# Bias rows formed on 128 partitions, and the indexer's narrow columns as one block, in a two-layer decoder trunk

## The chip, the cores and the metric

One Trainium2 chip, of which the program uses one core. The metric is the device time of one execution in microseconds. The time before is 1499.97 us, the median of three runs (1499.28 to 1501.76).

## The reference

Two post-norm layers on x of 256 tokens by 1024. Layer 0 mixes tokens with four heads of gated linear attention (GLA) and eight heads of sparse attention (DSA) whose keys an indexer selects, all from one input projection `w_in_ab`; a dense SwiGLU follows. Layer 1 mixes with forgetting attention and dilated attention, and ends in a top-2-of-8 expert SwiGLU. One table of relative biases (32 buckets by 8 heads) serves the DSA and the dilated heads. Cut to what the change touches:

```python
y = x @ w_in                                  # w_in_ab, 1024 x 3672
qa, ka, va, ra, ga, qb, kb, vb, qi, ki, wi = _split(y, AB_SPLITS)
g_log = jax.nn.log_sigmoid((ga @ w_gate + b_gate).astype(jnp.float32)) / GLA_GATE_TAU
...
score = jnp.einsum('bqh,bhqk->bqk', wib, jax.nn.relu(s))      # wi weighs the indexer's heads
...
bias = rel_table[_rel_bucket(tq[None, :, None] - sel)]
logits = logits + bias.transpose(0, 3, 1, 2).astype(jnp.float32)
```

Three of the parts of y are narrow: ga (16 columns, the gate's low rank), ki (64 columns, the indexer's key) and wi (8 columns, the weights of its heads). In the matrix, ki and wi stand side by side (columns 3600 to 3671); the second range that the kernel loads, columns 1512 to 1551, holds ga at its end (1536 to 1551), with 24 columns ahead of it that nobody uses.

## The kernel before

Every float32 projection is made from three matmuls (`mm3`, L188 to L190): weights and activations are each split in a high and a low half. `piece` (L151 and on) loads a block of weights into a ring of buffers named `raw` with a DMA on SP's queue, ScalarE casts it to the high half (`whi`, L160) and VectorE subtracts to get the low half (`wlo`, L162). Up to five such blocks are on their way in layer 0; a buffer comes free when the block's `wlo` is made, and the next load on SP's queue waits for that. `proj_t` makes 128 columns at a time: eight row blocks of 128, three matmuls each, so 24 matmuls of 256 columns for up to 128 weight columns.

`mixer_ab` is the first stage. In the order of its text: x is transposed, qa and ka are projected (a block of 1 MB for ka), `bias_tables` forms the bias rows, `router_weights` prepares something for the last stage, the narrow columns are projected, and then qb, qi, kb and va, interleaved with the GLA's scores, which need ga. The order in which each engine gets its instructions is made when the kernel is built, by a planner that simulates the time line; each engine then takes its instructions strictly in that order, DMA issues on its own queue among them.

`bias_tables` (L337 to L347) multiplies the table, 33 rows by 8 heads (`tb`), with a constant matrix (`oh`, 33 by 384 for each of two tables). The result has one row of 384 for each head, on 8 partitions (`row`, L346). L347 writes each row 32 times over to a buffer in DRAM (`scr_bias`), with one DMA on ScalarE's queue for each table. `bias_expand` (L356) reads it back later with four DMAs on ScalarE's queue, each row shifted by one element, into the tile `T`, which the DSA's logits add. `T` takes the place in SBUF of `oh` and `row` (tag `Tdsa`).

The narrow columns are fetched by two DMAs of L151: 72 columns (288 bytes a row) and 40 columns (160 bytes a row), for 1024 rows each, side by side in one ring buffer. `evac_small` takes ga, ki and wi out of the product.

Of the kernel before, what the change touches and what calls it, by code (L numbers as in the profile page):

```python
# [9 lines left out]
F32 = mybir.dt.float32  # L10
# [14 lines left out]
KT = 8  # L25
# [44 lines left out]

def layouts(inputs):

    cols = np.stack([inputs["ln_g"][1, 0], inputs["ln_b"][1, 0]]).reshape(2, KT, 128).transpose(2, 0, 1)
    return {"ln_cols": np.ascontiguousarray(cols)}


def drain(*gens):
    for g in gens:
        for _ in g:
            pass  # L80


def chain(*gens):
    for g in gens:
        yield from g


def interleave(main, side, n=1, m=1):

    alive = [True, True]  # L90
    while any(alive):
        for i, g, k in ((0, main, n), (1, side, m)):
            for _ in range(k):
                if alive[i] and next(g, g) is g:
                    alive[i] = False


def weave(pattern, **gens):

    for c in pattern:  # L100
        next(gens[c], None)


def lead(n, k):

    return [(t, i) for i in range(n - k) for t in range(NT)] + [(t, i) for t in range(NT) for i in range(n - k, n)]


class Trunk:
# [222 lines left out]

    def bias_tables(self, m):

        nc = self.nc
        tb = self.wk.tile([33, 8], F32, name="tb")
        nc.vector.memset(tb[32:33, :], 1.0)  # L337
        nc.gpsimd.dma_start(tb[0:32, :], self.io["rel_table"])
        both = m.tile([33, 2 * 768], F32, name="oh", tag="Tdsa")
        oh, row = both[:, 0:768], both[0:8, 768:2 * 768]  # L340
        nc.gpsimd.dma_start(oh, self.io["c_oh"])
        scr = self.dram.tile([8, 2, 32, 384], F32, name="scr_bias")
        for w in range(2):
            p = self.abank()
            nc.tensor.matmul(p[:8, :384], tb, oh[:, w * 384:(w + 1) * 384], start=True, stop=True)
            nc.vector.tensor_copy(row[:, w * 384:(w + 1) * 384], p[:8, :384])  # L346
            nc.scalar.dma_start(scr[:, w], row[:, None, w * 384:(w + 1) * 384].to_broadcast([8, 32, 384]))  # L347
        return scr

    def bias_expand(self, pool, scr, w, name):  # L350

        T = pool.tile([128, 8, 256], F32, name="T", tag=name)
        for p in range(0, 128, 32):
            src = bass.AP(tensor=scr.tensor, offset=scr.offset + w * 32 * 384 + 127 - p,
                          ap=[[383, 32], [2 * 32 * 384, 8], [1, 256]])
            self.nc.scalar.dma_start(T[p:p + 32], src)  # L356
        return T

# [252 lines left out]
    def mixer_ab(self, x):  # L611
        nc, io = self.nc, self.io
        w = io["w_in_ab"]
        with ExitStack() as st:
            pool = lambda n, b: st.enter_context(self.tc.tile_pool(name=n, bufs=b))
            self.wk, m = pool("wk0", 1), pool("m0", 1)
            self.pt = self.wk
            xT = self.pair(m, [128, KT, S], "xT")
            for t in range(NT):
                self.transposed(xT, x, t)  # L620
            qa, ka = (m.tile([128, 2, S], F32, name=n) for n in ("qa", "ka"))
            AT = m.tile([128, 2, 4, 128], F32, name="AT")
            AO = m.tile([128, 4, 128], F32, name="AO")
            sel = m.tile([128, 384], F32, name="sel")
            gaT = m.tile([16, S], F32, name="gaT")
            kw = m.tile([72, S], F32, name="kw")
            ki2 = m.tile([128, 1, S], F32, name="ki2")
            wiN = m.tile([128, NT, 8], F32, name="wiN")
            qi, qb, kb = (m.tile([128, 4, S], F32, name=n, tag="q4", bufs=5) for n in ("qi", "qb", "kb"))
            va, vb, sg = (m.tile([128, NT, 512], F32, name=n, tag="q4", bufs=5) for n in ("va", "vb", "sg"))  # L630
            oa = m.tile([128, NT, 512], F32, name="oa")
            drain(self.heads_t(w, 0, qa, xT, 0.125, step=1))
            self.constants()
            drain(self.heads_t(w, 256, ka, xT))
            scr = self.bias_tables(m)
            self.router_weights()

            def evac_small(p):

                nc.scalar.copy(gaT, p[96:112])  # L640
                nc.scalar.copy(kw, p[0:72])
                nc.vector.tensor_copy(ki2[0:64, 0], kw[0:64])
                nc.gpsimd.dma_start(ki2[64:128, 0], kw[0:64])
                for t in range(NT):
                    q = self.abank()
                    nc.tensor.transpose(q[:, 0:72], kw[:, t * 128:(t + 1) * 128], self.ident[:72, :72])
                    nc.vector.tensor_copy(wiN[:, t], q[:, 64:72])

            drain(self.proj_t([self.rows(w, 0, KT, 3600, 3672), self.rows(w, 0, KT, 1512, 1552)], [evac_small], xT))
            interleave(chain(self.heads_t(w, 1552, qb[:, 0:2], xT, 0.125),  # L650
                             self.heads_t(w, 3088, qi, xT),
                             self.dsa_select(qi, ki2, wiN, sel),
                             self.heads_t(w, 1808, qb[:, 2:4], xT, 0.125),
                             self.heads_t(w, 2064, kb, xT),
                             self.proj_n(w, 512, 512, xT, self.evac_n(va))),
                       self.gla_scores(gaT, qa, ka, AT, AO))
            T = self.bias_expand(m, scr, 0, "Tdsa")
            gn = m.tile([128, 128], F32, name="gn")
            nc.gpsimd.dma_start(gn, io["g_norm_a"].to_broadcast([128, 128]))
            oT = [m.tile([128, KT, S], F32R, name=n) for n in ("oTh", "oTl")]  # L660

            def logits(h, p, L):
                tm = self.wk.tile([128, 384], F32, name="tm", bufs=2)
                nc.gpsimd.tensor_add(tm[:, 0:128], T[:, h, 128:256], sel[:, 0:128])
                nc.gpsimd.tensor_add(tm[:, 128:384], T[:, h], sel[:, 128:384])
                nc.vector.tensor_add(L, p, tm)

            att = self.attention(qb, kb, vb, logits, oT, 4)
            last = self.out_proj(io["w_out_ab"], lambda k: [a[:, k] for a in oT], lead(4, 3), x, 0, 0)
            gate = self.gla_gate(oa, sg, gn, oT)  # L670
            weave("rgargarar", r=self.proj_n(w, 1024, 512, xT, self.evac_n(sg)),
                  g=self.gla_out(AT, AO, va, oa), a=att)
            weave("vgvgvvaaaaaaaa", v=self.proj_n(w, 2576, 512, xT, self.evac_n(vb)),
                  g=gate, a=att, o=last)
            drain(last)
        return scr
# [543 lines left out]
```

## Time and profile before

| | before |
|---|---|
| median of three runs | 1499.97 us |
| the profiled execution | 1500.22 us |
| its span, first to last instruction | 1498.4 us |
[...]
| TensorE matmul (PE) busy | 1461.3 us, 98% |
| TensorE weight load (PEld) busy | 1206.4 us, 81% |
| VectorE (DVE) busy | 1201.1 us, 80% |
| ScalarE (ACT) busy | 1025.9 us, 68% |
| GpSimd (POOL) busy | 63.2 us, 4% |
| DMA | 435.99 MB, 291 GB/s over the span |

"Busy" is the union of an engine's instructions; matmuls overlap their neighbours, and the pitch from one start to the next tells more than the length of one. An instruction's idle time stands in brackets with its releaser, the event that ended the wait. Queue q1 carries the DMAs of SP, q10 those of ScalarE. [...]

### The profile page before, as it was taken

The numbers are of one execution on the slowest core, as the hardware profiler recorded it, in microseconds if no ns is written. First come the engines' busy times: TensorE is split into PE (matmuls) and PEld (weight loads), VectorE is DVE, ScalarE is ACT, GpSimd is POOL, SyncE is SP. The second block draws the span as 40 slices with busy tenths as digits, with TensorE's granted clock in tenths as the row PEclk, the third lists the DMA queues.
The fourth block names the chain that finished last, engine by engine and source line by source line (L and its number), as shares of the span: only waits on it lengthen the run. The fifth ranks groups of instructions, "written<-read, shape, count | busy, mean of one in ns | idle before, by whom it ended". The sixth has DMA issues, their size and how long they took to land. (4 is left out here: it accounts for less than half of the span.)

```text
span 1498.4 us, 19533 instructions
## 1 busy us (share of the span) xinstructions
PE 1461.3 (98%) x7226; PEld 1206.4 (81%) x7226; DVE 1201.1 (80%) x1408; ACT 1025.9 (68%) x1328; POOL 63.2 (4%) x71
## 2 busy tenths in 40 slices
PE   6999899999999899999999999999999999999996
PEld 5987688888987788888888888888888887888885
DVE  3696564545645999999899999989889889889987
ACT  3647444433666787877778778787777777777764
POOL 1223000000100030000000000000000000000000
PEclk8999999999999999999999999999999999999998
DMA  8844565556546799999999999989999999999971
GB/s 223 254 141 137 200 199 195 177 189 199 181 141 225 264 321 392 388 357 361 357 331 372 376 357 369 374 325 351 370 337 356 359 353 329 370 365 359 362 262 58
DMA packets 199459, 435.99 MB, mean 291 GB/s; under 512 B 9298, under 2 KB 33658, under 8 KB 199360
## 3 DMA queue, kind: packets, MB, share of 16 engines
q1 hardware_dynamic: 195760, 429.88, 80.3%
q10 hardware_dynamic: 2848, 2.95, 1.1%
q0 software_dynamic: 752, 1.88, 0.4%
q8 instruction: 58, 0.95, 0.3%
q14 instruction: 41, 0.34, 0.1%
HBM read 432.77 MB, written 1.84 MB: 290 GB/s over the span
## 5 line engine op out<-in xcount | busy, mean ns | idle before, releaser
L162 DVE TENSOR_TENSOR wlo<-raw,whi 128x1024 fp32r<-128x1024 f32 (+1 forms) x811 | 962.1, 1222 | 151.5 <-ACT whi L160 131.6
L160 ACT CAST whi<-raw 128x1024 fp32r<-128x1024 f32 (+1 forms) x811 | 821.1, 1046 | 206.9 <-PE bank L190 132.0
L188 PE MATMUL bank<-whi,xgh 128*128 128x512 f32 x896 | 353.2, 395 | 0.0
L189 PE MATMUL bank<-wlo,xgh 128*128 128x512 f32 x896 | 352.4, 393 | 0.0
L190 PE MATMUL bank<-whi,xgl 128*128 128x512 f32 x896 | 351.2, 392 | 0.6 <-ACT xgl L912 0.6
L189 PEld LDWEIGHTS bank<-wlo,xgh 128*128 128x128 f32 x896 | 168.3, 188 | 40.4 <-DVE wlo L162 4.5
L190 PEld LDWEIGHTS bank<-whi,xgl 128*128 128x128 f32 x896 | 168.3, 188 | 36.7 <-ACT xgl L912 0.9
L188 PEld LDWEIGHTS bank<-whi,xgh 128*128 128x128 f32 x896 | 168.4, 188 | 35.7
L189 PE MATMUL y<-wlo,gTh 128*128 128x512 f32 x440 | 173.6, 395 | 0.0
L190 PE MATMUL y<-whi,gTl 128*128 128x512 f32 x440 | 171.4, 392 | 0.8 <-DVE gTl L183 0.8
L188 PE MATMUL y<-whi,gTh 128*128 128x512 f32 x440 | 149.0, 392 | 0.0
L190 PE MATMUL bank<-whi,xTl 128*128 128x512 f32 (+2 forms) x288 | 108.2, 377 | 3.8 <-DVE xTl L183 3.8
L188 PE MATMUL bank<-whi,xTh 128*128 128x512 f32 (+2 forms) x288 | 108.2, 377 | 2.6 <-ACT xTh L182 2.6
L189 PE MATMUL bank<-wlo,xTh 128*128 128x512 f32 (+2 forms) x288 | 107.6, 374 | 0.0
L190 PEld LDWEIGHTS y<-whi,gTl 128*128 128x128 f32 x440 | 82.6, 188 | 18.4 <-DVE gTl L183 1.2
L188 PEld LDWEIGHTS y<-whi,gTh 128*128 128x128 f32 x440 | 82.6, 188 | 18.0
L189 PEld LDWEIGHTS y<-wlo,gTh 128*128 128x128 f32 x440 | 82.7, 188 | 17.5 <-DVE wlo L162 0.2
L182 ACT CAST gTh<-abank 128x512 fp32r<-128x512 f32 (+1 forms) x67 | 38.8, 579 | 73.3 <-PE y L189 53.6
L188 PE MATMUL bank<-xTh,whi 128*128 128x256 f32 (+1 forms) x264 | 78.1, 296 | 6.6 <-ACT whi L160 6.6
L190 PE MATMUL bank<-xTh,wlo 128*128 128x256 f32 (+1 forms) x264 | 77.4, 296 | 0.7 <-DVE wlo L162 0.7
L189 PE MATMUL bank<-xTl,whi 128*128 128x256 f32 (+1 forms) x264 | 77.4, 293 | 0.0
L183 DVE TENSOR_TENSOR gTl<-abank,gTh 128x512 fp32r<-128x512 f32 (+1 forms) x67 | 45.4, 678 | 31.3 <-ACT gTh L182 31.3
(293 smaller groups left out, 1400.6 us busy)
## 6 DMA issues: line engine op xcount, KB each, us to landing
raw<-in_w_moe SPq DMA_DIRECT2D x333, 1024.0 KB, 6.5
raw<-in_w_dense SPq DMA_DIRECT2D x33, 1024.0 KB, 5.1
raw<-in_w_in_ab SPq DMA_DIRECT2D x13, 1024.0 KB, 12.5
raw<-in_w_in_cd SPq DMA_DIRECT2D x11, 1024.0 KB, 5.5
raw<-in_w_out_ab SPq DMA_DIRECT2D x4, 1024.0 KB, 4.8
raw<-in_w_out_cd SPq DMA_DIRECT2D x4, 1024.0 KB, 5.6
T<-scr_bias ACTq DMA_DIRECT2D x8, 256.0 KB, 5.5
raw<-in_w_moe SPq DMA_DIRECT2D x3, 512.0 KB, 4.2
```

Source lines behind the costliest of these rows:

```text
L160: nc.scalar.copy(hi, raw[:, sl])
L162: return lambda: nc.vector.tensor_sub(lo, raw[:, sl], hi.bitcast(F32))
L182: self.nc.scalar.copy(hi, src)
L183: self.nc.vector.tensor_sub(lo, src, hi.bitcast(F32))
L188: mm(out, a[0], b[0], start=start, stop=False, skip_group_check=True)
L189: mm(out, a[0], b[1], start=False, stop=False, skip_group_check=True)
L190: return mm(out, a[1], b[0], start=False, stop=stop, skip_group_check=True)
```

## The change

Two edits, both in layer 0's token mixer.

The bias rows. The table is first copied so that each head stands 16 times side by side (`many`, 33 by 128, one VectorE copy from a stride of zero). The matmul with it gives the same 384 numbers on 16 partitions for each head, 128 in all; the copy out of PSUM takes 128 partitions in place of 8; and each partition writes its row twice. The 32 copies of each row in DRAM are the same, but the two tables now lie one behind the other instead of alternating by head.

The narrow columns. The host lays the 112 columns out beforehand as an input of its own, `w_small`, 128 partitions by 8 blocks by 112 columns, so that each partition's part is one run of 3584 bytes; one DMA fetches it.

```diff
+    w = np.asarray(inputs["w_in_ab"][0])
+    small = np.concatenate([w[:, 3600:3672], w[:, 1512:1552]], axis=1).reshape(KT, 128, 112).transpose(1, 0, 2)
+    return {"ln_cols": np.ascontiguousarray(cols), "w_small": np.ascontiguousarray(small)}
...
-        both = m.tile([33, 2 * 768], F32, name="oh", tag="Tdsa")
-        oh, row = both[:, 0:768], both[0:8, 768:2 * 768]
+        both = m.tile([128, 2 * 768], F32, name="oh", tag="Tdsa")
+        oh, row = both[0:33, 0:768], both[:, 768:2 * 768]
         nc.gpsimd.dma_start(oh, self.io["c_oh"])
-        scr = self.dram.tile([8, 2, 32, 384], F32, name="scr_bias")
+        many = self.wk.tile([33, 8, 16], F32, name="tb16")
+        nc.vector.tensor_copy(many, tb[:, :, None].to_broadcast([33, 8, 16]))
+        scr = self.dram.tile([2, 8, 32, 384], F32, name="scr_bias")
         for w in range(2):
             p = self.abank()
-            nc.tensor.matmul(p[:8, :384], tb, oh[:, w * 384:(w + 1) * 384], start=True, stop=True)
-            nc.vector.tensor_copy(row[:, w * 384:(w + 1) * 384], p[:8, :384])
-            nc.scalar.dma_start(scr[:, w], row[:, None, w * 384:(w + 1) * 384].to_broadcast([8, 32, 384]))
+            nc.tensor.matmul(p[:, :384], many.rearrange("p h c -> p (h c)"), oh[:, w * 384:(w + 1) * 384],
+                             start=True, stop=True)
+            nc.vector.tensor_copy(row[:, w * 384:(w + 1) * 384], p[:, :384])
+            nc.scalar.dma_start(scr[w].rearrange("h (c b) n -> (h c) b n", b=2),
+                                row[:, None, w * 384:(w + 1) * 384].to_broadcast([128, 2, 384]))
...
-            src = bass.AP(tensor=scr.tensor, offset=scr.offset + w * 32 * 384 + 127 - p,
-                          ap=[[383, 32], [2 * 32 * 384, 8], [1, 256]])
+            src = bass.AP(tensor=scr.tensor, offset=scr.offset + w * 8 * 32 * 384 + 127 - p,
+                          ap=[[383, 32], [32 * 384, 8], [1, 256]])
...
-            drain(self.proj_t([self.rows(w, 0, KT, 3600, 3672), self.rows(w, 0, KT, 1512, 1552)], [evac_small], xT))
+            drain(self.proj_t(io["w_small"], [evac_small], xT))
```

## Rows read from the trace of the kernel before

**Rows 1.** Page, part 1: busy us, share of the span, instructions.

```profile
PE 1461.3 (98%) x7226; PEld 1206.4 (81%) x7226; DVE 1201.1 (80%) x1408; ACT 1025.9 (68%) x1328; POOL 63.2 (4%) x71
```

**Rows 2.** Waits of TensorE, 40 to 180 us, two of the four.

```profile
PE bank L190 <- DVE xTl L183: 2.6, 1, 2.6
PE abank L454 <- DVE AT L461: 1.0, 1, 1.0
```

**Rows 3.** Timeline of TensorE: start us, length us, operation, count, idle before, releaser.

```profile
21.53 0.39 PE L190 MATMUL bank<-xTh,wlo 128*128 128x256 f32 x1 [0.70 <-DVE wlo L162]
24.39 0.28 PE L189 MATMUL bank<-xTl,whi 128*128 128x256 f32 x1
31.26 0.55 PE L188 MATMUL bank<-xTh,whi 128*112 128x256 f32 x1 [6.59 <-ACT whi L160]
37.49 0.28 PE L188 MATMUL bank<-xTh,whi 128*112 128x256 f32 x1
39.15 0.28 PE L190 MATMUL bank<-xTh,wlo 128*112 128x256 f32 x1
```

**Rows 4.** Timeline of ScalarE and its queue, columns as in group 3.

```profile
17.59 1.99 ACT L160 CAST whi<-raw 128x1024 fp32r<-128x1024 f32 x2
30.64 1.03 ACT L160 CAST whi<-raw 128x448 fp32r<-128x448 f32 x2 [10.31 <-DMA raw<-in_w_in_ab]
36.41 1.84 ACTq L356 DMA_DIRECT2D T<-scr_bias  x4
```

**Rows 5.** DMA issues, 0 to 50 us: KB each, median us to landing.

```profile
raw<-in_w_in_ab SPq DMA_DIRECT2D x1, 288.0 KB, 16.4
raw<-in_w_in_ab SPq DMA_DIRECT2D x1, 160.0 KB, 19.2
scr_bias<-oh ACTq DMA_DIRECT2D x2, 384.0 KB
```

**Rows 6.** DMA by queue, 24 to 29 us: packets, MB, share of 16 engines.

```profile
q10 hardware_dynamic: 158, 0.24, 44.0%
q1 hardware_dynamic: 128, 0.02, 2.2%
```

**Rows 7.** Windows: length, busy us (count) of PE, PEld, DVE, ACT, POOL; PEclk, DMA.

```profile
26.00:27.00 1.00, 0.00 (x0) 0.00 (x0) 0.00 (x0) 0.00 (x0) 0.00 (x0) 1.00 0.47 53
27.00:28.00 1.00, 0.00 (x0) 0.00 (x0) 0.00 (x0) 0.00 (x0) 0.00 (x0) 0.56 0.48 54
36.00:37.00 1.00, 1.00 (x7) 1.00 (x6) 1.00 (x2) 0.73 (x2) 0.00 (x0) 0.50 1.11 350
37.00:38.00 1.00, 1.00 (x9) 1.00 (x9) 0.91 (x1) 0.00 (x0) 0.00 (x0) 0.82 1.11 350
```

**Rows 8.** DMA by queue, 12 to 14 us.

```profile
q1 hardware_dynamic: 682, 0.72, 109.2%
```

**Rows 9.** Groups of TensorE, 31.26 to 39.26 us: count, busy us, mean ns.

```profile
L190 PE MATMUL bank<-xTh,wlo 128*128 128x256 f32 (+1 forms) x16 | 5.4, 365 | 0.0
L188 PE MATMUL bank<-xTh,whi 128*112 128x256 f32 (+1 forms) x14 | 5.3, 377 | 6.6 <-ACT whi L160 6.6
L189 PE MATMUL bank<-xTl,whi 128*112 128x256 f32 (+1 forms) x14 | 5.1, 364 | 0.0
```

**Rows 10.** DMA by queue, 1493 to 1498 us (the output's writes, from 128 partitions).

```profile
q1 hardware_dynamic: 576, 1.05, 56.4%
```

**Rows 11.** Timeline of VectorE and TensorE's weight load at the bias matmuls.

```profile
9.93 0.13 PEld L345 LDWEIGHTS abank<-oh,tb 33*8 33x8 f32 x1 [0.51 <-issue]
11.88 0.54 DVE L346 COPY oh<-abank 8x384 f32<-8x384 f32 x1
```

**Rows 12.** Page, part 5, a weight load of 128 columns: busy us, mean ns.

```profile
L189 PEld LDWEIGHTS bank<-wlo,xgh 128*128 128x128 f32 x896 | 168.3, 188 | 40.4 <-DVE wlo L162 4.5
```

**Rows 13.** Windows before and in the key selection; columns as in group 7.

```profile
40.00:76.00 36.00, 36.00 (x324) 33.82 (x322) 25.56 (x39) 23.70 (x37) 9.63 (x13) 1.00 0.78 242
76.00:108.00 32.00, 30.98 (x224) 26.35 (x222) 30.91 (x84) 15.46 (x27) 4.32 (x7) 1.00 0.37 128
```

More of the change, by code (lines that the diff above doesn't have):

```diff
@@ L73, in layouts @@
     cols = np.stack([inputs["ln_g"][1, 0], inputs["ln_b"][1, 0]]).reshape(2, KT, 128).transpose(2, 0, 1)
-    return {"ln_cols": np.ascontiguousarray(cols)}
+    w = np.asarray(inputs["w_in_ab"][0])
+    small = np.concatenate([w[:, 3600:3672], w[:, 1512:1552]], axis=1).reshape(KT, 128, 112).transpose(1, 0, 2)
+    return {"ln_cols": np.ascontiguousarray(cols), "w_small": np.ascontiguousarray(small)}
 def drain(*gens):
```

## The prediction, made before the changed kernel was run

> **What bounds the kernel now.** I read the page first, then TensorE's waits, then its timeline at the longest of them. TensorE is busy for 1461.3 us, 98% of the span [rows 1], so almost any hole in its work is time of the whole kernel. After 40 us it hardly waits: from 40 to 180 us, the rest of layer 0's mixer, four waits add up to 5.1 us, two of which are shown [rows 2]. The largest hole stands before. TensorE starts a matmul at 24.39 us and the next at 31.26 us, after 6.59 us of idling [rows 3]. The releaser is ScalarE's cast L160, and that cast had itself waited 10.31 us for a DMA into `raw` [rows 4]. The cast is 448 elements wide (half of 8 x 112), so it is that of the narrow columns. Its first matmuls stand in TensorE's order ahead of the last of ka, and hold ka's back too.
>
> Why does the block come so late? Its two DMAs took 16.4 and 19.2 us to land, for 288 and 160 KB [rows 5]. They are not slow by their bytes: from 24 to 29 us q1, their queue, has 128 packets to its name, which took 2.2% of the engines' time, while q10, ScalarE's, moves 158 packets and holds 44.0% [rows 6]. The 158 packets are 0.24 MB, so 1536 bytes each, one row of biases: these are the writes to `scr_bias`, 384 KB each [rows 5]. 44% of 16 engines is 7.0 engines' time: about half of the engines sit in these writes, and the narrow columns' rows on those engines come out between them, about one for one. The other engines are idle; that is the DMA share of 0.47 at 53 GB/s [rows 7].
>
> The hole costs twice. [...]
>
> **The change, part by part.**
>
> *The hole.* 6.59 us go if the block is there in time. In time means: the cast began 0.62 us before the matmul that it released (30.64 and 31.26), and ka's last unblocked matmul ends at 24.67 (24.39 + 0.28) [rows 3, 4], so the cast must begin by 24.05. It can't begin before ka's casts end, at 19.58 (17.59 + 1.99) [rows 4]. For the data I count generously: at 14 us, with all of ka's 1.05 MB still to come, the block's 0.46 MB and both writes' 0.79 MB, 2.30 MB in all, at the 0.72 MB in 2 us that q1 moved from 12 to 14 [rows 8], take 6.4 us and end at 20.4. That leaves 3.6 us for the completion. What is late next is the block after it (1.05 MB for qb, 2.9 us more, 23.3 us): TensorE gets to it only at 29.8 (24.67 + 5.10, below), so it hides.
>
> *The clock.* From 31.26 to 39.15 TensorE starts 44 matmuls [rows 3, 9] (16 + 14 + 14), that is 43 pitches in 7.89 us. At full clock the 15 matmuls from 37.49 to 39.15 (first and last shown [rows 3]) have 14 pitches in 1.66 us, 0.1186 us each. 43 of them are 5.10 us, so 2.79 us more go. That there is no drop without the hole I take from the wait of 0.70 us at 21.53 [rows 3], which left the clock alone.
>
> *The bias rows.* The writes are as many bytes and packets as before (512 of 1536), but from 128 partitions. How fast a write from 8 partitions is, the trace shows: 158 packets in 5 us, 32 a us [rows 6]. From 128 partitions there is only the output's write: 576 packets and 1.05 MB, for 56.4% of 16 engines over 5 us, so 45 us of an engine, 23 KB in each [rows 10]. At that, 0.79 MB cost 34 us of an engine, 2.1 us on 16; at the old rate 16 us. These are the ends, and they are far apart. I take the first, since 128 partitions to DRAM is what the change does; the second is a rival below.
>
> [...]
>
> *Small additions.* `many` is one VectorE copy of 128 elements a partition; the nearest row is the copy of 384, 0.54 us [rows 11]. It takes between 0 and that, early, when TensorE still waits for qa's weights. The four weight loads of the bias matmuls take 128 columns in place of 8: between 0.13 [rows 11] and 0.188 us [rows 12], 0.2 us for all four. The matmuls move the same 384 columns, and the copy of the result is as long per partition. I put all this at nothing; without its cover it would be 0.8 us. On SP's queue one issue goes, and all loads behind it move up, as far as their buffers are free. On ScalarE's queue the two writes stay two issues, and `bias_expand`'s four, 1.84 us from 36.41 [rows 4], read rows that are written earlier than now. `T`'s first reader comes in the attention, long after.
>
> *What the gain meets later.* VectorE is busy 30.91 of 32 us from 76 to 108, but TensorE is too, with 30.98, and before it VectorE has 10 us to spare in 36 [rows 13]. All of that work hangs on the projections ahead of it, so it moves as one piece. I expect nothing given back.
>
> The sum: 6.59 + 2.79 = 9.38 us. The profiled execution took 1500.22 us (span 1498.4 and 1.8 around it), 0.25 above the median of 1499.97. 1500.22 - 9.38 = **1490.8 us**.
>
> **The rivals.**
>
> *The writes are bound by DRAM, not by their 8 partitions.* Then 512 packets at 32 a us hold all 16 engines from about 14 to 30 us. Packets of q1 go one for one with them as in [rows 6], 32 a us: the block's 128 take 4 us, and it is there by about 21, in time. But of qb's 1024 rows of 1 KB only some 280 pass by 30 us; the other 740 at 341 a us [rows 8] end at 32.2, and a cast and a subtraction (1.0 and 1.2 us) later, near 34, TensorE goes on, having nothing from 29.8. Some 4 us are lost again, and if the clock falls another 2.8: 1494.4 to 1497.2, say 1496. For it: the trace has no quick write of rows to this buffer in 24 to 29 us. Against it: the output's rate, and about half the engines idle.
>
> *It goes, and comes back in the order.* The planner makes the order anew with other durations. If it pulls GLA and selection work ahead, VectorE, which has 1 us to spare in 32 [rows 13], makes TensorE wait for `wlo` pieces of about 1.2 us; four to nine such waits return half or all of the gain: 1495 to 1501, say 1499. The same time holds if the block isn't early because something else in SP's queue holds it.
>
> *Slower.* The four issues of `bias_expand` stand on ScalarE's queue behind ka's evacuation, at 36.41 [rows 4], and wait there for the writes. If the planner, believing the writes short, puts them ahead of ka's casts (17.59), and the writes on the chip still end near 30, ScalarE stands still for 12 us, and TensorE starts all of ka and the narrow columns, 72 matmuls, at about 31. The first 29 go at the slow pitch (31.26 to 37.49, 0.215 each, 6.2 us), 43 at 0.1186 (5.1): it ends at 42.3 in place of 39.3, 3 us late, and T's 1 MB then goes beside the weights of qb and qi, for 1 more: 1504. It decides once the issues stand before the casts and the writes end after about 27 us.
>
> **How the numbers follow.** Forecast 0.64 (1488 to 1493.5: the planner's order, and 2 us of the remaining waits [rows 2] either way); DRAM-bound writes 0.14; given back in the order 0.14; slower 0.08. About 0.2%, 3 us, is what a measurement of this kernel tells from no change. Below 1497: 0.64, the 0.14 of the second but for a little, and 0.05 of the third, 0.82. Within 3 us: 0.10. Above 1503: 0.08. The range for 8 in 10 takes in the first two cases and a little of the third: 1488 to 1497.5.
>
> **What would show it.** In the changed trace the hole before the matmuls of the narrow columns is gone or under 1 us; the granted clock stays at 1.00 from 17 to 40 us; the last matmul of the narrow columns starts near 29.8 in place of 39.15; q10's packets are through by about 20 us with a share that goes to all 16 engines; and the stages behind, the key selection and the experts' first matmul, begin 9 us earlier. I am wrong if the block's cast begins after 24 us, if TensorE waits for qb, or if `bias_expand` stands ahead of casts on ScalarE's queue with idle time behind it.

## The result, and the profile after

The changed kernel takes 1490.67 us (median of six runs, 1488.71 to 1491.18), the kernel before 1500.12 us (six runs, 1498.03 to 1502.69). The ratio of the means is 0.9934, with an interval of 0.9921 to 0.9947. Between the medians that is 9.45 us less, and 1490.8 us had been forecast. The profiled execution of the changed kernel took 1491.18 us, with a span of 1489.3 us. Its mean granted clock, what the throttle lets TensorE run at as a share of full speed, was 0.989; in the profiled execution before it was 0.987.

Part 1 of the page of the changed kernel answers [rows 1]:

```profile
PE 1457.5 (98%) x7226; PEld 1205.2 (81%) x7226; DVE 1202.3 (81%) x1409; ACT 1026.0 (69%) x1328; POOL 63.8 (4%) x71
```

TensorE has the same 7226 instructions and the same share of a shorter span; VectorE has one instruction more, the copy into `many`.

TensorE's timeline of the changed kernel answers [rows 3] (lines 188 to 190 are now 191 to 193):

```profile
21.86 0.39 PE L193 MATMUL bank<-xTh,wlo 128*128 128x256 f32 x1 [0.70 <-DVE wlo L165]
24.83 0.28 PE L191 MATMUL bank<-xTh,whi 128*112 128x256 f32 x1
29.96 0.28 PE L193 MATMUL bank<-xTh,wlo 128*112 128x256 f32 x1
```

The first matmul of the narrow columns starts at 24.83 us with no idle time before it, and their last at 29.96 instead of 39.15. The 6.59 us are gone; the 0.70 us before 21.86 are the only idle time that is left between 20 and 42 us.

ScalarE's timeline of the changed kernel answers [rows 4]:

```profile
17.92 1.99 ACT L163 CAST whi<-raw 128x1024 fp32r<-128x1024 f32 x2
20.55 1.02 ACT L163 CAST whi<-raw 128x448 fp32r<-128x448 f32 x2
22.29 2.00 ACT L163 CAST whi<-raw 128x1024 fp32r<-128x1024 f32 x2 [0.72 <-DMA raw<-in_w_in_ab]
26.55 1.39 ACTq L364 DMA_DIRECT2D T<-scr_bias  x3
```

The narrow columns' cast (448 elements) begins at 20.55 and waits for nothing, where it had waited 10.31 us. The cast of qb's weights behind it waits 0.72 us. The reads of `T` are still issued after all of ka's casts, three at 26.55 and the fourth at 28.00.

The DMA view of the changed kernel, by queue (packets, MB, share of 16 engines), from 15 to 21 us, and two of its issues from 0 to 50 us (KB each, median us to landing), answer [rows 5, 6]:

```profile
q1 hardware_dynamic: 1270, 1.54, 71.4%
q10 hardware_dynamic: 544, 0.79, 35.0%
...
scr_bias<-oh ACTq DMA_DIRECT2D x2, 384.0 KB, 6.7
raw<-in_w_small SPq DMA_DIRECT2D x1, 448.0 KB, 9.2
```

All 0.79 MB of the bias rows pass in these 6 us, and beside them q1 moves 1.54 MB of weights. 35.0% of 16 engines over 6 us is 33.6 us of an engine; for 512 packets of 1536 bytes (the other 32 are small) that is 66 ns a packet. Before, 44.0% over 5 us were 35.2 us for 158 packets, 223 ns each [rows 6].

### The profile page after: what moved, and what is told of

It reads as the page before. It is cut to its first block, busy times and chain, and to the rows that moved or that the text cites. A ratio compares the mean times of both kernels' runs of the same rounds, so it can differ in the third digit from the quotient of the medians.

```text
span 1489.3 us, 19533 instructions
## 1 busy us (share of the span) xinstructions
PE 1457.5 (98%) x7226; PEld 1205.2 (81%) x7226; DVE 1202.3 (81%) x1409; ACT 1026.0 (69%) x1328; POOL 63.8 (4%) x71
```

## The experiments

Five variants were run to part the change's two edits, to separate the number of partitions from their place, and to price the hole; three more to look at what is left. The first three below and the first one with the router's weights later ran beside 1499.54 us of the kernel before (16 runs), the others beside 1499.6 us (14 runs).

### The rows on 128 partitions alone

The changed kernel, with the narrow columns again as two DMAs:

```diff
-            drain(self.proj_t(io["w_small"], [evac_small], xT))
+            drain(self.proj_t([self.rows(w, 0, KT, 3600, 3672), self.rows(w, 0, KT, 1512, 1552)], [evac_small], xT))
```

> The bias rows on 128 partitions alone; the narrow columns stay two DMAs of 288 and 160 bytes a row. My theory is that the writes of the bias rows hold half of the engines and that the narrow rows only queue behind them: then nearly the whole gain is here, 1490.5 to 1492 us, TensorE's hole before the narrow columns is under 1 us and the clock does not fall there. The rival is that the short rows themselves are slow: then their cast still begins after 27 us and the time is 1497 to 1500.

Measured: 1489.46 us (1489.03 to 1493.09), ratio 0.9938, interval 0.9924 to 0.9951, 1 us below the range that was expected. ScalarE's timeline of this variant, and its DMA by queue from 15 to 19 us:

```profile
20.10 1.03 ACT L163 CAST whi<-raw 128x448 fp32r<-128x448 f32 x2 [0.32 <-DMA raw<-in_w_in_ab]
```
```profile
q1 hardware_dynamic: 1952, 0.55, 60.9%
q10 hardware_dynamic: 544, 0.79, 54.8%
```

The two DMAs with rows of 288 and 160 bytes make the cast wait 0.32 us, and it still begins at 20.10, well ahead of need. The writes cost 35 us of an engine as in the changed kernel (54.8% of 16 over 4 us). The whole gain is that of the rows' partitions; the block isn't needed for it.

The 1952 packets of q1 above average 280 bytes, and take 20 ns of an engine each (60.9% of 16 engines over 4 us). That is 14 bytes a ns, where the 1 KB packets of the next variant move 22 (9.3% of 16 over 5 us for 161). The short packets are slower by the byte here, and cost the kernel nothing that these runs can tell, because the cast has time (20.10, where 24.05 would do).

### The block alone

The kernel before, with the narrow columns' block in DRAM and one DMA for it; the bias rows stay on 8 partitions:

```diff
-            drain(self.proj_t([self.rows(w, 0, KT, 3600, 3672), self.rows(w, 0, KT, 1512, 1552)], [evac_small], xT))
+            drain(self.proj_t(io["w_small"], [evac_small], xT))
```

> The narrow columns as one block alone; the bias rows are written from 8 partitions as before. By my theory the block, with 8 packets on each engine that stand between packets of the writes (0.22 us each), still lands by about 19 to 21 us, but the block for qb, 64 packets on each engine, is held back until the writes end near 30 us: TensorE meets a hole of 3 to 4 us ahead of qb instead, with or without a fall of the clock (2.8 us). That gives 1494 to 1497.5. If the short rows were the cause, the whole gain would be here: 1490.7.

Measured: 1499.81 us (1497.17 to 1501.31), ratio 0.9998, interval 0.9989 to 1.0007. No gain, where 1494 to 1497.5 had been expected. ScalarE's timeline of this variant:

```profile
19.79 1.02 ACT L163 CAST whi<-raw 128x448 fp32r<-128x448 f32 x2
31.18 1.04 ACT L163 CAST whi<-raw 128x1024 fp32r<-128x1024 f32 x1 [10.37 <-DMA raw<-in_w_in_ab]
...
40.09 2.00 ACT L163 CAST whi<-raw 128x1024 fp32r<-128x1024 f32 x2 [3.21 <-DMA raw<-in_w_in_ab]
46.16 1.05 ACT L163 CAST whi<-raw 128x1024 fp32r<-128x1024 f32 x1 [3.80 <-DMA raw<-in_w_in_ab]
```

The block is there in time (19.79, no wait). But qb's block, next in SP's queue, makes its cast wait 10.37 us, and later blocks come late as well. The DMA by queue of this variant from 24 to 29 us says why:

```profile
q10 hardware_dynamic: 159, 0.24, 42.0%
q1 hardware_dynamic: 161, 0.16, 9.3%
```

The writes hold about the share of [rows 6], 42.0% beside 44.0%, and q1's packets, of 1 KB now, pass one for one with them: 161 beside 159. All of TensorE's idle times from 28 to 56 us in this variant, and the windows around them (PEclk is the third number from the end):

```profile
32.27 0.58 PE L191 MATMUL bank<-xTh,whi 128*128 128x256 f32 x1 [2.80 <-ACT whi L163]
33.53 0.58 PE L193 MATMUL bank<-xTh,wlo 128*128 128x256 f32 x1 [0.47 <-DVE wlo L165]
52.55 1.13 PE L441 MATMUL abank<-sq,ls_o 128*128 128x256 f32 x2 [2.47 <-DVE ls_o L422]
```
```profile
33.00:39.00 6.00, 5.53 (x26) 5.47 (x26) 4.24 (x5) 3.44 (x7) 0.56 (x1) 0.50 1.10 278
53.00:56.00 3.00, 3.00 (x14) 2.46 (x14) 2.36 (x2) 1.76 (x3) 0.00 (x0) 0.50 1.05 388
```

The hole has moved from the narrow columns to qb and shrunk to 3.27 us, with some 6 us at a granted clock of 0.50 behind it. Then a second hole of 2.47 us opens at 52.55, in GLA, again with the clock at 0.50 afterwards. Its releaser is VectorE's `ls_o`; VectorE had to wait 1.60 us for ScalarE, whose last late cast runs from 47.59 to 48.64 us and whose `ls_a` comes behind it, at 49.11 and 51.05:

```profile
51.80 0.69 DVE L422 SCALAR_TENSOR_TENSOR ls_o<-ls_o,ls_a 128x512 f32<-128x512 f32 x1 [1.60 <-ACT ls_a L421]
```

The holes are 5.74 us instead of 6.59, and TensorE works at the low clock behind both of them, where it did behind one before. That this eats the 0.85 us is argued and not shown: a fall of the clock as short as the second also comes in traces without a hole (below, under the clock). Without the quick writes, an early block only hands the delay to the next load in the queue.

### Eight rows, on every fourth partition

The kernel before, with eight rows as there, on partitions 0, 4, ..., 28 instead of 0 to 7. Each head's row is formed four times, on 32 partitions, and only the first of the four is written; it is still written 32 times by its own partition, and the narrow columns stay two DMAs:

```diff
+            many = self.wk.tile([33, 8, 4], F32, name="tb4")
+            nc.vector.tensor_copy(many, tb[:, :, None].to_broadcast([33, 8, 4]))
...
-            nc.scalar.dma_start(scr[:, w], row[:, None, w * 384:(w + 1) * 384].to_broadcast([8, 32, 384]))
+            nc.scalar.dma_start(scr[:, w],
+                                row[0:32:4, None, w * 384:(w + 1) * 384].to_broadcast([8, 32, 384]))
```

> The kernel before, with the 8 bias rows on partitions 0, 4, 8 to 28 in place of 0 to 7 (each head formed four times, the first of them written); eight partitions and eight rows as before, the narrow columns as two DMAs as before. If it is the place of the partitions that slows the writes, not their number, a packet of 1536 bytes takes 0.07 to 0.11 us in place of 0.22, the writes end by about 20 to 23 us, and the time is 1490.5 to 1492.5. [...] If one partition can give only so much, or the DRAM takes only so much from 8 engines, the packets stay at 0.22 us and the time at 1500.

Measured: 1492.46 us (1489.7 to 1495.34), ratio 0.9961, interval 0.9949 to 0.9974. Its DMA by queue from 17 to 20 us, and ScalarE's timeline:

```profile
q1 hardware_dynamic: 846, 0.52, 58.7%
q10 hardware_dynamic: 339, 0.51, 45.0%
```
```profile
21.32 1.03 ACT L160 CAST whi<-raw 128x448 fp32r<-128x448 f32 x2 [1.63 <-DMA raw<-in_w_in_ab]
```

45.0% of 16 engines over 3 us are 21.6 us of an engine for 339 packets, 64 ns each, where 158 packets from partitions 0 to 7 took 223 [rows 6]: as quick as from 128 partitions (66), with as few source partitions as before, the same packets and the same DRAM rows. So the slow packets of before were a matter of where the eight partitions lie, not of how many there are, nor of DRAM. Nor do the quick writes hold more of the DMA engines' time while they last: 45.0% of 16 is 7.2 engines' time, as before (7.0). The cast begins at 21.32, before the 24.05 of the prediction, and TensorE's timeline has no hole there (its one wait for ka's and the narrow columns' weights is 0.7 us, for `wlo`).

Its median is 3 us above that of the 128 partitions alone, and the two intervals meet at 0.9949 to 0.9951. Its fastest run, the profiled one at 1489.7 us, had a mean granted clock of 0.992, its slowest, at 1495.34, one of 0.988. Whether it is really slower than 128 partitions stays open.

### The hole put back, in two sizes

The changed kernel, with the block's load moved to GpSimd's queue and held back there by a chain of 3 (or 5) tiny loads into the same buffer. So the writes are quick, and only the narrow columns are late:

```diff
+        held, self.held = getattr(self, "held", 0), 0
+        for _ in range(held):
+            nc.gpsimd.dma_start(raw[:, 0, 0:8], self.io["ln_cols"][:, 0])
...
-            nc.sync.dma_start(raw[:, :, c:c + s.shape[2]], s)
+            (nc.gpsimd if held else nc.sync).dma_start(raw[:, :, c:c + s.shape[2]], s)
...
+            self.held = 3
             drain(self.proj_t(io["w_small"], [evac_small], xT))
```

> The changed kernel with the block's load held back by a chain of three tiny loads on GpSimd's queue (each waits for the one before), nothing else taken away: the writes stay quick and all loads on SP's queue stay early. The planner now puts the block's casts behind ka's evacuation, so ka ends near 27.4 us. I expect the block at 29 to 32 us and a hole of 2 to 5 us. By my theory the time is that of the changed kernel plus the hole, plus up to 2.8 us where the clock falls in it: 1492.5 to 1498.5. The rival is that the gain came with the quicker loads on SP's queue and not from the hole: then 1490.7 whatever the hole.

> The same with five tiny loads: the block at 37 to 44 us, a hole of 10 to 17 us and a fallen clock after it (2.8 us): 1503 to 1510. By the rival 1490.7. If the hole grows between the two by more than the time does, something else hides a part of it.

> The changed kernel once more, as the measure for the three beside it: 1490 to 1491.5 us. What is open: in its first trace the granted clock fell to 0.50 near 38 us, for 3.4 us, with TensorE at work and no hole. If that falls with the order of the instructions, it is there again at the same place; if not, it is elsewhere or gone, and the time moves by 1 to 2 us with it.

Measured: with three, 1498.89 us (1496.34 to 1502.08), ratio 0.9998, interval 0.9988 to 1.0007. With five, 1506.67 us (1505.63 to 1508.6), 1.0054, interval 1.0039 to 1.0068. The changed kernel beside them: 1489.8 us (1488.5 to 1490.33), 0.9937, interval 0.9922 to 0.9951. TensorE's timeline of the variant with three and then of the one with five:

```profile
34.23 0.56 PE L194 MATMUL bank<-xTh,whi 128*112 128x256 f32 x1 [7.30 <-ACT whi L166]
```
```profile
40.30 0.56 PE L194 MATMUL bank<-xTh,whi 128*112 128x256 f32 x1 [13.75 <-ACT whi L166]
```

The holes came out larger than meant, since a tiny load took 5.7 us from issue to landing with three and 5.0 with five (medians). But they price the hole: 7.30 us cost 9.1 us (1498.89 - 1489.8), 13.75 cost 16.9 (1506.67 - 1489.8). The hole is paid in full, and 1.8 and 3.1 us more with it; the spread of the runs leaves, by an estimate from it, some 1.5 us of doubt on each. The clock came back to 1.00 in these windows, with three and then with five:

```profile
37.00:38.00 1.00, 1.00 (x9) 1.00 (x9) 1.00 (x2) 1.00 (x2) 0.00 (x0) 0.82 0.94 294
```
```profile
46.00:47.00 1.00, 1.00 (x7) 1.00 (x7) 1.00 (x2) 0.97 (x2) 0.00 (x0) 0.68 1.10 348
```

So TensorE worked some 3 and 6 us at the low clock behind its holes, and the variant that worked longer at it paid more beyond the hole; with five, the clock also falls between 53 and 57 us (0.57 in that window) without a hole. Quick writes alone gain nothing if the narrow columns still come late.

### The router's weights later

TensorE's wait of 0.70 us at 21.86 stands before ka's low half. The changed kernel, with the loading and splitting of the router's weights moved behind the narrow columns:

```diff
-            self.router_weights()
             ...
             drain(self.proj_t(io["w_small"], [evac_small], xT))
+            self.router_weights()
```

> The changed kernel, with router_weights called after the narrow projection instead of before it. In the changed kernel VectorE holds ka's low halves behind a reduction of router_weights (L333) that waits for a small matmul in TensorE's order, and TensorE waits 0.70 us for the low half. I expect this wait gone and 0.5 to 1.3 us less than the changed kernel: 1489.4 to 1490.2. The rival is that the small matmuls and reductions cost the same where they now stand, among the projections of qb: 1490.7.

Measured: 1489.28 us (1488.34 to 1490.33), ratio 0.9937, interval 0.9923 to 0.995. TensorE's waits in this variant up to 40 us, leaving out one of 4.5 us at the very start that the changed kernel has too:

```profile
PE bank L191 <- ACT whi L163: 0.9, 1, 0.9
PE bank L193 <- DVE wlo L165: 0.2, 1, 0.2
```

The 0.70 us are gone, as expected, and up to 40 us nothing came in their place: these two stand among qa's matmuls, at 10.69 and 11.42, where the changed kernel waits 1.65 us at 11.41. (Behind 40 us there is a new wait of 0.3 us, for `ls_o`.) But 0.7 us are too little to be told from the runs: the ratio of the changed kernel is 0.9934 and, in the second series, 0.9937. Last, the rows on 128 partitions with two narrow DMAs and the router's weights later:

> The bias rows on 128 partitions, the narrow columns as two DMAs as before, and router_weights after the narrow projection: the edits that the first runs left as carrying the gain. If the block adds nothing, as the run with the rows alone says, this is as fast as the changed kernel with router_weights later, 1488.5 to 1490 us; if the block is worth 1 us, 1490 to 1491.

Measured: 1487.38 us (1486.5 to 1489.66), ratio 0.9922, interval 0.9908 to 0.9936. It is the lowest median of all, 1 us below the range that was expected, and four of its five runs lie below all five of the changed kernel beside it. But the two intervals overlap (0.9922 to 0.9951 there), and its trace shows no term of that size: the 0.70 us at ka are gone, and a wait of 0.7 us for `ls_o` has come behind 40 us. So it isn't shown to be better.

## Why the prediction was right

*The writes.* The term on which all hung was 34 us of an engine for both writes, read from the output's rate; they took 33.6. The rival, writes bound by DRAM, is excluded by the changed kernel (0.79 MB within 6 us) and by the eight spread rows, which go to the same DRAM rows. Its mechanism is real all the same: the block alone shows it, with packets one for one (161 beside 159) and qb late (10.37 us at its cast). There 4 us of hole were reckoned for qb, and 3.27 measured; what was missing was the second hole in GLA, of 2.47 us, behind ScalarE's late casts. (The rival's lower end, 1494.4, lies 0.4 us below its own terms, 1490.8 + 4; nothing hangs on it.) That the place of the eight partitions decides, and not their number (223 ns a packet and 64), is what the eight spread rows add; the prediction's sum didn't need it.

*In time or not.* The cast had to begin by 24.05 and began at 20.55 (forecast for the data: 20.4). qb's data were there at 22.29 (forecast 23.3), and TensorE didn't wait for them.

*The hole.* 6.59 us were forecast to go, and went. The two holes put back confirm that it is paid in full.

*The clock.* Before, the granted clock was 1.00 from 26 to 27 us, in the hole, 0.56 in the next window, and still 0.50 from 36 to 37, behind the hole [rows 7]. The term of 2.79 us is right where it was read: the last matmul of the narrow columns starts at 29.96 (forecast 29.8), 9.19 us earlier. The step behind it, that the clock doesn't fall without the hole, failed. Windows of the changed kernel:

```profile
27.00:28.00 1.00, 1.00 (x11) 1.00 (x10) 0.00 (x0) 0.01 (x1) 0.00 (x0) 1.00 1.10 348
37.00:38.00 1.00, 1.00 (x9) 1.00 (x10) 0.90 (x2) 0.59 (x1) 0.00 (x0) 0.96 1.12 251
38.00:39.00 1.00, 1.00 (x7) 1.00 (x6) 0.33 (x1) 0.79 (x1) 0.00 (x0) 0.50 1.12 271
40.00:41.00 1.00, 1.00 (x7) 1.00 (x7) 0.52 (x1) 0.98 (x2) 0.00 (x0) 0.50 1.10 352
```

From 38 us the granted clock is 0.50 for some 3 us, with TensorE at work and no idle time since 21.86. Of the 9.19 us, 8.20 are left behind it (the key selection, too, starts 7.99 us earlier, with VectorE's first MAX8 at 83.05 instead of 91.04, where 9 had been forecast), in the same pair of matmuls of the mixer's output projection, first before, then after:

```profile
151.44 0.73 PE L190 MATMUL bank<-whi,oTl 128*128 128x512 f32 x2
```
```profile
143.24 0.73 PE L193 MATMUL bank<-whi,oTl 128*128 128x512 f32 x2
```

What is lost there comes back at the layer norm that follows, where TensorE idles in both kernels (the longest wait is 2.63 us in each, for `xTl`, up to 171.22 before and 163.03 after) and the clock falls. Windows of that stretch, before and after, and the experts' first matmuls, before and after:

```profile
170.00:177.00 7.00, 5.78 (x14) 4.52 (x15) 4.78 (x9) 2.53 (x3) 0.56 (x1) 0.53 1.04 380
```
```profile
164.00:168.00 4.00, 4.00 (x12) 3.11 (x12) 2.62 (x5) 2.25 (x3) 0.56 (x1) 0.57 1.02 373
```
```profile
501.62 0.39 PE L188 MATMUL bank<-whi,xgh 128*128 128x512 f32 x1
```
```profile
492.13 0.40 PE L191 MATMUL bank<-whi,xgh 128*128 128x512 f32 x1
```

At the low clock stand some 7 us before and 3.5 after, and the changed kernel leads by 9.49 at the experts (501.62 - 492.13) and by 9.1 over the whole span (1498.4 - 1489.3). So the sum of 9.38 holds in this execution with two clock effects of about 1 us each that offset one another, and neither of them was in it: that part of the agreement is luck. A second execution of the changed kernel shows that they don't belong to the program. Its windows, and two of its matmuls:

```profile
38.00:39.00 1.00, 1.00 (x10) 1.00 (x10) 1.00 (x2) 0.80 (x2) 0.00 (x0) 1.00 1.11 350
...
160.00:165.00 5.00, 4.77 (x11) 3.81 (x12) 3.78 (x8) 2.53 (x3) 0.56 (x1) 0.50 1.03 380
```
```profile
20.53 0.39 PE L193 MATMUL bank<-xTh,wlo 128*128 128x256 f32 x1 [0.70 <-DVE wlo L165]
489.80 0.39 PE L191 MATMUL bank<-whi,xgh 128*128 128x512 f32 x1
```

Here nothing falls at 38 us, and the layer norm's stretch at the low clock is longer instead. The whole took 1488.5 us. The experts start at 489.80, another 2.33 us ahead of the first execution. 1.33 of these stand already at the first matmul shown (20.53 instead of 21.86): ahead of it the granted clock was 0.51 from 14 to 15 us and 1.00 in the next window, while in the first execution it was 0.50 until 17 us and 0.78 from 17 to 18.

The fall without a hole is no exception, though. The rows alone, the router's weights later, and both together have no hole either, and their windows are, in this order:

```profile
37.00:39.00 2.00, 2.00 (x11) 2.00 (x11) 1.23 (x1) 1.00 (x2) 0.00 (x0) 0.50 1.12 264
```
```profile
36.00:38.00 2.00, 2.00 (x11) 2.00 (x11) 0.00 (x0) 1.07 (x2) 0.00 (x0) 0.50 1.10 343
```
```profile
35.00:37.00 2.00, 2.00 (x11) 2.00 (x11) 0.60 (x2) 0.00 (x0) 0.00 (x0) 0.50 1.12 269
```

So of five traces with the rows on 128 partitions and no hole, four have this fall, at 34 to 38 us. By the holes put back, which cost 1.8 and 3.1 us beyond their length, the 2.79 for the clock's share of a hole is of the right size, within the doubt on those two.

*Given back in the order; slower.* Neither happened. The experts start 9.49 us earlier, so nothing came back. The four issues of `bias_expand` moved from 36.41 to 26.55 and 28.00, behind ka's casts; the planner did not put them ahead.

*Small additions.* The copy into `many` took 0.35 us on VectorE, at 5.88, and the copies of the bias rows 0.55 instead of 0.54 [rows 11]:

```profile
5.88 0.35 DVE L347 COPY tb<-tb 33x128 f32<-33x128 f32 x1 [4.91 <-DMA tb<-in_rel_table]
12.00 0.55 DVE L353 COPY oh<-abank 128x384 f32<-128x384 f32 x1
```

They lie under work as assumed. What the prediction did not part was the change's two edits: it let the block be part of the gain, and the rows alone do it all.

## What to carry to other kernels

When a load is late, look at which queue holds the DMA engines while it is under way, by share of engines and not by bytes: a write of 0.79 MB on another queue here held 44.0% of the engines' time [rows 6], and the cast of a load of 0.46 MB waited 10.31 us [rows 4]. Before buying speed with more partitions or larger descriptors, spread the few partitions that there are; every fourth of 32 was as quick per packet here as all 128 (64 and 66 ns). And ask of each cure what is next in the same queue: the block alone made the narrow columns early (their cast at 19.79), and the next load took their place (its cast waited 10.37 us).

## What was not expected of the hardware

A write of eight rows took 223 ns a packet of 1536 bytes from partitions 0 to 7, 64 from 0, 4, ..., 28 and 66 from 128, each beside loads on SP's queue.

The granted clock fell to 0.50 for some 3 us at 38 us in one execution of the changed kernel, with TensorE at work and without a hole, and not in another execution of the same program; three other variants without a hole have it between 34 and 37 us. What sets it off wasn't found. Runs of one kernel differ roughly with their mean granted clock: 1496.34 us at 0.992 and 1502.08 at 0.986 with the chain of three, 1486.5 at 0.994 and 1489.66 at 0.989 with the rows and the router's weights later; but 1489.18 at 0.989 and 1489.28 at 0.992 with the router's weights later alone. The experts start at 492.13 in one execution of the changed kernel and at 489.80 in the other. So a single profile places a point of this kernel's time line to some 2 us, and its total no better than the spread of 2 to 6 us between runs.
